# Hybrid decoder layer on one core: other waiting steps in the attention and ahead of the decay products, the keys' rate term on another engine, two small products in other banks

## The chip, the cores and the metric

The kernel runs on one core of a Trainium2 chip. The metric is the device time of one execution in microseconds (us); the time of a kernel is the median of its runs.

## The reference

A layer of width 2048 works on one sequence of 256 tokens in fp32. A first SwiGLU block of width 5632 is followed by a mixer, a cross attention into a memory of 256 tokens, a second SwiGLU block and a final norm. The mixer runs two token mixers beside each other, gates them and projects the sum:

```
h = rms_norm(x, norm_g)
p = h @ w_in
q, k, v, p_rwkv, gates = jnp.split(p, c, axis=-1)
y_attn = sliding_window_attention(q, k, v, sinks)
y_rwkv = rwkv7_time_mix(p_rwkv, mu, w0, w2, a0, a2, g2, k_k, k_a, r_k, ln_w, ln_b)
gate_attn, gate_rwkv = jnp.split(jax.nn.sigmoid(gates), 2, axis=-1)
merged = gate_attn * (y_attn @ w_proj_attn) + gate_rwkv * (y_rwkv @ w_proj_rwkv)
return x + merged @ w_out
```

The attention has 16 heads in four groups (`kv` 0 to 3), each group with one key and value head, a window of 128 tokens and a sink. In the RWKV-7 part the change touches the decay, the rate `a` and the keys:

```
w_log = -jax.nn.softplus(-(w0 + jnp.tanh(xw) @ w2)) - 0.5
a = jax.nn.sigmoid(a0 + xa @ a2)
g = jax.nn.sigmoid(xg) @ g2
kk = k * k_k
kk = kk / jnp.maximum(jnp.sqrt(jnp.sum(kk * kk, axis=-1, keepdims=True)), 1e-12)
k = k * (1.0 + (a - 1.0) * k_a)
```

The last line holds the keys' rate term, `1 + (a - 1) k_a`.

## The kernel before, in words

Every large product takes fp32 operands in two parts, hi and lo, and is done as three products of a faster form (lines L442 to L444 in `times`: hi·hi, lo·hi, hi·lo). Weights stream in through SyncE's queue (SP) as tiles `raw`; ScalarE (ACT) casts the hi part (L365) and VectorE (DVE) subtracts the lo part (L366), both in the order in which TensorE (PE) uses them. This stream is the backbone of the kernel.

All other work stands in generators. After each `multiply` (six of those products on one bank) the function `product` calls `bg.tick()`, and each waiting generator does its piece up to its next `yield`. Such a piece is a step; `idle(n)` lets n steps pass. Generators stand in groups with a limit: of the group "attn" two run at a time, of "ew" one. On top of this the build layer arranges the rows of each engine by its own estimates.

PSUM has three tags: `acc` (three banks, the stream's sums), `mm` (three) and `tr` (two, for transposes and small products). A row that writes a bank waits until ACT or DVE has emptied it.

The places of the change, in order of the program:
- `attend(kv)`, L938 to L1030, once for each head group: scores (L954, in `tr` and `mm`), bias and maximum on DVE (L962, L974), exponentials on ACT (L984), their normalising on DVE (L993), transposes on PE (L1003), copies of them on ACT (L1007, `pt`), the product with the values on PE (L1014), and its split into hi and lo (L1024 on ACT, L1025 on DVE). It idles at L945 before the scores and at L996 before the transposes.
- `decay_and_rate`, L1072 to L1130: when the attention has been issued, GpSimd (POOL) starts two DMAs for the weights `wa` (L1078, L1079); ACT does the tanh of `xwa` and the sigmoid of `xg` (L1081, L1082); PE then does two blocks of eight products per bank tag (L1091) and ACT their sigmoids (L1098).
- `gate_parts`, L1141: three copies of a part of `xg` by DMA, also issued by POOL (L1144).
- `removal_keys(h)`, L1163 to L1232, for two halves h: `kk` scaled on ACT (L1172), normalised on DVE (L1184, L1186), the products with decay and rate (L1190 to L1197), the keys' rate term (L1202), its use (L1206, L1207), products (L1216) and their masking (L1224).
- The gates: ACT's sigmoid (L1268), and DVE's product `ga` (L1271), which empties an `acc` bank of the stream.
- The RWKV pairs: masked scores (`mk`, L1348 on PE, L1356 on DVE); the bank taken at L1449 holds the products of L1459 to L1472. `finish` (L1486 to L1534) takes a bank for the product with the gate's weights, L1523.

Of the kernel before, what the change touches and what calls it, by code (L numbers as in the profile page):

```python
# [9 lines left out]
AF = mybir.ActivationFunctionType  # L10
ALU = mybir.AluOpType
# [125 lines left out]
def decoder_layer(ctx: ExitStack, tc: tile.TileContext, a: dict, out: bass.AP):  # L137
    nc = tc.nc
    act, dve, pool, pe = nc.scalar, nc.vector, nc.gpsimd, nc.tensor
# [17 lines left out]
    def f32(x):  # L157
        return x.bitcast(F32)
# [4 lines left out]
    def mm():  # L163
        return ps.tile([P, 512], F32, tag="mm", name="mm")

    def tr():
        return ps.tile([P, 512], F32, tag="tr", name="tr", bufs=2)
# [5 lines left out]
    def idle(n):  # L173
        for _ in range(n):
            yield
# [68 lines left out]
    w0, a0, k_k, k_a, r_k, ln_w, ln_b = (cols[:, 80 + i * 8 : 88 + i * 8] for i in range(7))  # L244
    mu = cols[:, 136:163]
    nk_k = cpool.tile([P, 8], F32, name="nk_k")
    ok_a = cpool.tile([P, 8], F32, name="ok_a")
# [22 lines left out]
    for entry in weight_plan(a):  # L270
# [10 lines left out]
        for k in range(k0, k0 + nk, 2 * KU):  # L281
            u = len(units)
            units += [(v, k + i, c, 512) for v, c in zip(w, c0) for i in (0, KU)]
            for i in range(2):
                q = (k - k0) // KU + i
# [587 lines left out]
    with tc.tile_pool(name="mx", bufs=1, reuse_waits="tile") as sp:  # L873
# [66 lines left out]
        def attend(kv):  # L940
            yield from wait_for("kv")
            if kv == 0:
                with tc.issue_after(at["features"].ins):
                    act.activation(junk_t[:, :1], ones[:, :1], AF.Exp)
            yield from idle(5 * (kv % 2))  # L945
            s, b = [], []
            for qb, bank in enumerate((tr, mm)):
                w, tq = P * (qb + 1), slice(qb * P, qb * P + P)
# [9 lines left out]
            for qb in range(2):  # L958
                w = P * (qb + 1)
                bias = abias[:, 1 - qb :, :].rearrange("p a b -> p (a b)")  # L960
# [30 lines left out]
            for qb in range(2):  # L991
                for i in range(4):
                    dve.tensor_scalar(  # L993
                        s3[qb][:, i], s3[qb][:, i], den[:, qb, i : i + 1], None, ALU.mult
                    )
            yield from idle(3)  # L996
            pt = []
            for qb in range(2):
                pt.append(t4("pt", (P, 2, 4, P)))
# [71 lines left out]
        cs, ee, e0, aa, at_, bt, dec = [], [], [], [], [], [], []  # L1071
        keep2 = keep[:].rearrange("p c t -> p (c t)")  # L1072

        def decay_and_rate():
            yield from wait_for("small")
            yield from wait_for("attn")
            wa = t4("wa", (P, RW))
            pool.dma_start(wa[0:64, :], W["rwkv_w2"])  # L1078
            pool.dma_start(wa[64:128, :], W["rwkv_a2"])  # L1079
            with tc.issue_after(at["exp"].ins):  # L1080
                act.activation(xwa[0:64, :], xwa[0:64, :], AF.Tanh)  # L1081
                act.activation(xg[:], xg[:], AF.Sigmoid)  # L1082
            yield
            for h in range(2):
                cs.append(t4("cs"))
                aa.append(t4("aa"))
                b = [[bank() for _ in range(2)] for bank in (mm, tr)]
                for i in range(4):
                    for e in range(2):
                        r, c = slice(64 * e, 64 * e + 64), (4 * h + i) * P  # L1090
                        pe.matmul(  # L1091
                            b[i // 2][e][:, i % 2 * T : (i % 2 + 1) * T], wa[r, c : c + P],
                            xwa[r, :], start=True, stop=True,
                        )
                for i in (2, 3, 0, 1):
                    for e, (dst, bias) in enumerate(((cs[h], w0), (aa[h], a0))):
                        c = 4 * h + i
                        sigmoid = act.activation(  # L1098
                            dst[:, i, :], b[i // 2][e][:, i % 2 * T : (i % 2 + 1) * T], AF.Sigmoid,
                            bias=bias[:, c : c + 1],  # L1100
                        )
                yield from idle(4)
            for h in range(2):
                for c in range(4):
                    dve.tensor_tensor_scan(
                        cs[h][:, c, :], keep2, cs[h][:, c, :], 0.0, ALU.mult, ALU.add
                    )
                    if c % 2:
                        yield
                c3 = halves(cs[h])  # L1110
                mid = stat.tile([P, 8], F32, tag="mid", name="mid")
                dve.tensor_copy(mid[:], c3[:, :, 63])
                dve.tensor_tensor(
                    c3, c3, mid[:].unsqueeze(2).to_broadcast([P, 8, P]), ALU.subtract
                )
                dec.append(stat.tile([P, 4], F32, tag="dec", name="dec"))
                dve.tensor_tensor(dec[h][:], cs[h][:, :, 127], mid[:, 1:8:2], ALU.add)
                yield
                with tc.issue_after(sigmoid.ins):
                    act.activation(dec[h][:], dec[h][:], AF.Exp, scale=-DECAY)  # L1120

                ee.append(t4("ee", (P, 8, P)))
                e0.append(stat.tile([P, 8], F32, tag="e0", name="e0"))
                with tc.issue_after(sigmoid.ins):
                    act.activation(e0[h][:], mid[:], AF.Exp, scale=DECAY)
                    act.activation(ee[h][:], c3, AF.Exp, scale=-DECAY)
                yield
                act.activation(cs[h][:], cs[h][:], AF.Exp, scale=DECAY)
                yield
            bg.seen.add("decay")  # L1130
# [34 lines left out]
        def removal_keys(h):  # L1165
            yield from wait_for(f"k{h}")
            yield from wait_for("decay")
            ei = cs[h]
            kk, sq = t4("kk"), t4("sq")
            for i in range(4):  # L1170
                c = 4 * h + i
                act.activation(kk[:, i, :], kt[h][:, i, :], AF.Copy, scale=nk_k[:, c : c + 1])  # L1172
            yield
            act.activation(sq[:], kk[:], AF.Square)
            yield
            for i in (0, 2):
                b = tr()
                sq2 = sq[:, i : i + 2, :].rearrange("p c t -> p (c t)")
                pe.matmul(b[:], bdones[:], sq2, start=True, stop=True)
                act.activation(sq2, b[:], AF.Sqrt)  # L1180
                yield
                dve.tensor_scalar(sq2, sq2, 1e-12, None, ALU.max)
                for k in range(2):
                    dve.reciprocal(sq[:, i + k, :], sq[:, i + k, :])  # L1184
                    yield from idle(2)
            dve.tensor_tensor(kk[:], kk[:], sq[:], ALU.mult)  # L1186
            yield
            at_.append(t4("at"))
            for later, before in ((slice(1, P), ee[h][:, :, : P - 1]), (0, e0[h][:])):
                dve.scalar_tensor_tensor(  # L1190
                    halves(at_[h])[:, :, later], halves(kk)[:, :, later], DOWN, before,
                    ALU.mult, ALU.mult,
                )
            yield
            dve.scalar_tensor_tensor(kk[:], kk[:], -1.0, aa[h][:], ALU.mult, ALU.mult)
            yield
            dve.tensor_tensor(kk[:], kk[:], ei[:], ALU.mult)  # L1197
            bt.append(kk)
            yield
            for i in range(4):  # L1200
                c = 4 * h + i
                dve.tensor_scalar(  # L1202
                    aa[h][:, i, :], aa[h][:, i, :], k_a[:, c : c + 1], ok_a[:, c : c + 1],
                    ALU.mult, ALU.add,
                )
            dve.tensor_tensor(kt[h][:], kt[h][:], aa[h][:], ALU.mult)  # L1206
            dve.tensor_tensor(aa[h][:], kt[h][:], ei[:], ALU.mult)  # L1207

            lt = t4("lt", (P, 8, P))
            b = [[bank() for _ in range(2)] for bank in (tr, mm)]  # L1210
            for c in range(2):
                cs_ = slice(c * P, (c + 1) * P)
                for j in range(4):
                    for e in range(2):
                        r = slice(64 * e, 64 * e + 64)
                        pe.matmul(  # L1216
                            b[c][e][:, j * P : (j + 1) * P], at_[h][r, j, cs_], bt[h][r, j, cs_],
                            start=True, stop=True,
                        )
            for c in range(2):  # L1220
                lt = lt if c == 0 else t4("lt", (P, 8, P))
                yield
                for e in range(2):
                    dve.tensor_tensor(  # L1224
                        lt[:, 4 * e : 4 * e + 4, :], b[c][e][:].rearrange("p (j s) -> p j s", j=4),
                        mask_l[:].unsqueeze(1).to_broadcast([P, 4, P]), ALU.mult,
                    )
                o = h * 16 + c * 8
                pool.dma_start(ld[:, o : o + 8, :], lt[:])
                yield  # L1230
            yield
# [131 lines left out]
        def pairs(h, q):  # L1363
# [11 lines left out]
            for c in range(2):  # L1375
# [9 lines left out]
                b = tr()  # L1385
# [13 lines left out]
                b = tr()  # L1399
# [29 lines left out]
                if c == 0:  # L1429
                    b = mm()  # L1430
# [15 lines left out]
                if c == 0:  # L1446
                    mk_next = masked(scores(h, js, ((0, 1), (1, 1)), tr), mask3[:, :2])
                    yield
                b = tr()  # L1449
                if c:  # L1450
                    for k, j in enumerate(js):
                        pe.matmul(
# [36 lines left out]
        def finish(h, i):  # L1489
# [16 lines left out]
            b = head_sums(bdmean, sp_)  # L1506
# [6 lines left out]
            gl = sp.tile([P, 2 * P], F32R, tag="gl", name="gl", bufs=1)  # L1513
            dve.tensor_tensor(gl[:], g2[:, 0, :], f32(gh[:, 0]), ALU.subtract)
            dve.tensor_tensor(gh[:64, 1], g2[:64, 1, :], f32(gh[:64, 1]), ALU.subtract)
            yield from idle(2)
            b = tr()
            for k in range(2):
                o, fk = b[:, k * T : (k + 1) * T], slice(k * P, (k + 1) * P)
                for m, (g_, x_) in enumerate((  # L1520
# [132 lines left out]
        for h in (0, 2):  # L1653
            b = tr()
# [129 lines left out]
```

## Time and profile before

| | us |
|---|---|
| median of 3 runs | 2225.18 (2224.05 to 2226.93) |
| profiled execution | 2226.33 |
| its span | 2224.6 |
| PE busy | 2206.0 |
| DVE busy | 1831.3 |
| ACT busy | 1244.2 |
| POOL busy | 107.2 |

The profile is of one execution, so numbers from it go with 2226.33; 1.73 us of that lie around the span. Busy time counts an engine as busy however slow its clock; PE's granted clock has a column of its own in the views of windows. A row of a timeline gives start, duration, engine, line, what is written and read, and in brackets the idle time ahead of it with what ended it.

### The profile page before, as it was taken

The numbers are of one execution on the slowest core, as the hardware profiler recorded it, in microseconds if no ns is written. First come the engines' busy times: TensorE is split into PE (matmuls) and PEld (weight loads), VectorE is DVE, ScalarE is ACT, GpSimd is POOL, SyncE is SP. The second block draws the span as 40 slices with busy tenths as digits, with TensorE's granted clock in tenths as the row PEclk, the third lists the DMA queues.
The fourth block names the chain that finished last, engine by engine and source line by source line (L and its number), as shares of the span: only waits on it lengthen the run. The fifth ranks groups of instructions, "written<-read, shape, count | busy, mean of one in ns | idle before, by whom it ended". The sixth has DMA issues, their size and how long they took to land.

```text
span 2224.6 us, 28133 instructions
## 1 busy us (share of the span) xinstructions
PE 2206.0 (99%) x10520; PEld 1819.2 (82%) x10520; DVE 1831.3 (82%) x2354; ACT 1244.2 (56%) x1611; POOL 107.2 (5%) x185
## 2 busy tenths in 40 slices
PE   9999999999999999999999999999999999999998
PEld 7888888888888877788888888888888888888886
DVE  7999988898989476978657666558999999999997
ACT  7555555555556467544544546556665565655654
POOL 0000000000000001000221030001000000000000
PEclk9999999999999999999999999999999999999999
DMA  8565555555556545676678678548565565656573
GB/s 304 194 209 198 194 203 199 201 191 202 203 192 202 175 126 149 191 235 209 205 236 293 203 265 281 186 157 288 206 234 189 197 247 204 208 208 218 199 242 137
DMA packets 231560, 466.02 MB, mean 209 GB/s; under 512 B 15520, under 2 KB 17920, under 8 KB 231424
## 3 DMA queue, kind: packets, MB, share of 16 engines
q1 hardware_dynamic: 222256, 438.08, 58.0%
q0 software_dynamic: 7648, 23.52, 3.5%
q10 hardware_dynamic: 1520, 2.63, 0.3%
q8 instruction: 82, 1.34, 0.2%
q14 instruction: 54, 0.44, 0.1%
HBM read 440.49 MB, written 23.59 MB: 209 GB/s over the span
## 4 chain that ended last, share of the span: by engine, by line
PE 94%; DVE 2%; DMA 1%; issue 1%; ACT 1%; SPq 0%; POOL 0%; POOLq 0%; DVEq 0%; ACTq 0%
PE acc L442 19%; PE acc L443 19%; PE acc L444 19%; PE mm L443 8%; PE mm L444 8%; PE mm L442 8%; PE tr L443 2%; PE tr L630 2%; PE tr L442 2%; PE tr L444 2%; PE mm L1418 1%; DVE lo L366 1%; DMA raw<-in_ffn_w_up_dram 0%; ACT hi L365 0%; DMA raw<-in_ffn_w_gate_dram 0%
## 5 line engine op out<-in xcount | busy, mean ns | idle before, releaser
L365 ACT CAST hi<-raw 128x1024 fp32r<-128x1024 f32 (+1 forms) x768 | 754.9, 993 | 698.3 <-PE acc L444 493.6
L366 DVE TENSOR_TENSOR lo<-raw,hi 128x1024 fp32r<-128x1024 f32 (+1 forms) x768 | 880.7, 1150 | 291.7 <-ACT hi L365 288.9
L442 PE MATMUL acc<-hi,xhi 128*128 128x512 f32 (+1 forms) x1134 | 448.1, 396 | 2.8 <-DVE ga L1271 1.3
L443 PE MATMUL acc<-lo,xhi 128*128 128x512 f32 (+1 forms) x1134 | 440.6, 389 | 0.8 <-DVE lo L366 0.8
L444 PE MATMUL acc<-hi,xlo 128*128 128x512 f32 (+1 forms) x1134 | 440.5, 389 | 0.0
L442 PEld LDWEIGHTS acc<-hi,xhi 128*128 128x128 f32 x1134 | 213.3, 188 | 49.2 <-issue 3.6
L443 PEld LDWEIGHTS acc<-lo,xhi 128*128 128x128 f32 x1134 | 213.6, 188 | 44.2 <-DVE lo L366 2.1
L444 PEld LDWEIGHTS acc<-hi,xlo 128*128 128x128 f32 x1134 | 213.2, 188 | 44.1 <-issue 0.8
L373 ACT CAST thi<-raw 128x1024 fp32r<-128x1024 f32 x192 | 200.2, 1051 | 67.5 <-DVE raw L396 44.1
L374 DVE TENSOR_TENSOR tlo<-raw,thi 128x1024 fp32r<-128x1024 f32 x192 | 232.5, 1219 | 0.9 <-ACT thi L373 0.3
L442 PE MATMUL mm<-hi,xhi 128*128 128x512 f32 x402 | 156.5, 389 | 0.0
L443 PE MATMUL mm<-lo,xhi 128*128 128x512 f32 x402 | 156.5, 389 | 0.0
L444 PE MATMUL mm<-hi,xlo 128*128 128x512 f32 x402 | 156.4, 389 | 0.0
L444 PE MATMUL acc<-hi,hlo 128*128 128x512 f32 x372 | 145.4, 391 | 0.0
L443 PE MATMUL acc<-lo,hhi 128*128 128x512 f32 x372 | 145.3, 391 | 0.0
L442 PE MATMUL acc<-hi,hhi 128*128 128x512 f32 x372 | 145.0, 390 | 0.0
L442 PEld LDWEIGHTS mm<-hi,xhi 128*128 128x128 f32 x402 | 75.5, 188 | 16.2 <-ACT hi L365 0.5
L443 PEld LDWEIGHTS mm<-lo,xhi 128*128 128x128 f32 x402 | 75.5, 188 | 15.8
L444 PEld LDWEIGHTS mm<-hi,xlo 128*128 128x128 f32 x402 | 75.5, 188 | 15.7
L442 PEld LDWEIGHTS acc<-hi,hhi 128*128 128x128 f32 x372 | 69.9, 188 | 14.3
L443 PEld LDWEIGHTS acc<-lo,hhi 128*128 128x128 f32 x372 | 69.8, 188 | 14.2
L444 PEld LDWEIGHTS acc<-hi,hlo 128*128 128x128 f32 x372 | 69.9, 188 | 14.1
(421 smaller groups left out, 3527.9 us busy)
## 6 DMA issues: line engine op xcount, KB each, us to landing
raw<-in_ffn_w_down_dram SPq DMA_DIRECT2D x88, 1024.0 KB, 5.2
raw<-in_ffn_w_gate_dram SPq DMA_DIRECT2D x84, 1024.0 KB, 5.0
raw<-in_ffn_w_up_dram SPq DMA_DIRECT2D x78, 1024.0 KB, 5.9
raw<-in_w_in_dram SPq DMA_DIRECT2D x136, 512.0 KB, 3.7
raw<-in_w_out_dram SPq DMA_DIRECT2D x32, 512.0 KB, 4.6
raw<-sums SPq DMA_DIRECT2D x20, 512.0 KB, 6.3
raw<-in_w_proj_attn_dram SPq DMA_DIRECT2D x16, 512.0 KB, 4.1
raw<-in_w_proj_rwkv_dram SPq DMA_DIRECT2D x16, 512.0 KB, 5.3
```

What stands on the lines that cost most here:

```text
L365: at["hi"] = act.copy(hi[:, s], raw[:, s])
L366: at["lo"] = dve.tensor_tensor(lo[:, s], raw[:, s], f32(hi[:, s]), ALU.subtract)
L373: act.copy(hi[:], v[:])
L374: dve.tensor_tensor(lo[:], v[:], f32(hi[:]), ALU.subtract)
L442: pe.matmul(o, xh, hi, start=first, stop=False, **how)
L443: pe.matmul(o, xh, lo, start=False, stop=False, **how)
L444: pe.matmul(o, xl, hi, start=False, stop=last, **how)
L630: pe.transpose(b[:, o : o + P], tok[:, t, col : col + P], ident[:])
L1418: pe.matmul(vb[to, (o + k) * P : (o + k + 1) * P][:, r], lhs(k, e), v[:, k, r], start=v is u and k + e == 0, stop=True, **ek,)
```

## The change

Five edits:
- The fourth head group (`kv` 3) no longer idles five steps before its scores; the second still does.
- The first head group idles five steps instead of three before its transposes.
- After the two DMAs for `wa`, five steps pass before the tanh, the sigmoid and the products.
- The keys' rate term is done by ACT (Identity with scale and bias), four operations per half, instead of by DVE.
- Two small products take an `mm` bank instead of `tr`: at L1449 for one pair, at L1517 for the first `finish`, which also idles one step instead of two.

```
-            yield from idle(5 * (kv % 2))
+            yield from idle(5 * (kv == 1))
...
-            yield from idle(3)
+            yield from idle(5 if kv == 0 else 3)
...
             pool.dma_start(wa[64:128, :], W["rwkv_a2"])
+            yield from idle(5)
             with tc.issue_after(at["exp"].ins):
...
-                dve.tensor_scalar(
-                    aa[h][:, i, :], aa[h][:, i, :], k_a[:, c : c + 1], ok_a[:, c : c + 1],
-                    ALU.mult, ALU.add,
+                act.activation(
+                    aa[h][:, i, :], aa[h][:, i, :], AF.Identity, scale=k_a[:, c : c + 1],
+                    bias=ok_a[:, c : c + 1],
                 )
...
-                b = tr()
+                b = mm() if h == q == 1 and c == 0 else tr()
...
-            yield from idle(2)
-            b = tr()
+            yield
+            b = mm() if h == i == 0 else tr()
```

One line is added, so the lines of the changed kernel from L1080 on stand one number higher.

How the rows move, first on POOL, around the requests for `wa`; a row is line, operation, what is written and read, and the shape:

```order
 L1040 MEMSET p 128x2 x2
-L1144 DMA xg<-xg 32x256 x2
+L1145 DMA xg<-xg 32x256
 L1078 DMA wa<-in_rwkv_w_dram 64x1024
 L1079 DMA wa<-in_rwkv_a_dram 64x1024
+L1145 DMA xg<-xg 32x256 x2
 L1047 TENSOR_TENSOR d<-p 128x512 x2
-L1144 DMA xg<-xg 32x256
 L1040 MEMSET p 128x2 x2
```

One copy of `xg` stands ahead of the requests instead of two, and the other two follow them.

Then ACT, from the third head group's exponentials to the sigmoid of `xg`. Before:

```order
L984 ACTIVATE s,den<-s,nm 128x128 x3
L984 ACTIVATE s,den<-s,nm 128x256 x4
L1024 CAST yahi<-tr 128x512
L365 CAST hi<-raw 128x1024 x2
...
L365 CAST hi<-raw 128x1024 x2
L981 ACTIVATE es<-es 128x8
L984 ACTIVATE s,den<-s,nm 128x128 x4
L984 ACTIVATE s,den<-s,nm 128x256 x4
L365 CAST hi<-raw 128x1024 x2
L1007 COPY pt<-tr 128x512
L1081 ACTIVATE xwa<-xwa 64x256
L1082 ACT_TABLE_LOAD
```

And now:

```order
L984 ACTIVATE s,den<-s,nm 128x256 x4
L365 CAST hi<-raw 128x1024 x2
L1007 COPY pt<-tr 128x512
L984 ACTIVATE s,den<-s,nm 128x128
L981 ACTIVATE es<-es 128x8
L984 ACTIVATE s,den<-s,nm 128x128 x3
L984 ACTIVATE s,den<-s,nm 128x256 x4
L1007 COPY pt<-tr 128x512 x2
L365 CAST hi<-raw 128x1024
L1082 ACTIVATE xwa<-xwa 64x256
L1024 CAST yahi<-tr 128x512
L1083 ACT_TABLE_LOAD
```

The fourth group's exponentials now stand between the first and the other two of the third group's copies of transposed weights.

Last, DVE in the first half of the removal keys, from the product with the decay to `ga`. Before:

```order
L1197 TENSOR_TENSOR kk<-kk,cs 128x1024
L1202 TENSOR_SCALAR aa<-aa,cols,ok_a 128x256 x4
L366 TENSOR_TENSOR lo<-raw,hi 128x1024
L1206 TENSOR_TENSOR kt<-kt,aa 128x1024
L1224 TENSOR_TENSOR lt<-tr,mask_l 128x512
L1207 TENSOR_TENSOR aa<-kt,cs 128x1024
L1224 TENSOR_TENSOR lt<-tr,mask_l 128x512
L1224 TENSOR_TENSOR lt<-mm,mask_l 128x512 x2
L1271 TENSOR_TENSOR ga<-acc,ga 128x512 x2
```

And now:

```order
L1198 TENSOR_TENSOR kk<-kk,cs 128x1024
L1207 TENSOR_TENSOR kt<-kt,aa 128x1024
L366 TENSOR_TENSOR lo<-raw,hi 128x1024
L1208 TENSOR_TENSOR aa<-kt,cs 128x1024
L1225 TENSOR_TENSOR lt<-tr,mask_l 128x512 x2
L1225 TENSOR_TENSOR lt<-mm,mask_l 128x512 x2
L1272 TENSOR_TENSOR ga<-acc,ga 128x512 x2
```

The four operations of the rate term are gone from DVE, and `ga` stands that much earlier. On PE the first product into the bank that the second `ga` empties stood behind 13 products of the next tile pair into the other bank, and stands behind 7 now. PE does the same 9989 operations; the eight decay products of the first block keep their place in its order.

## The prediction

> **What bounds the kernel now.** I read the page first, then the list of PE's waits, then windows around the longest of them.
>
> ```profile
> PE 2206.0 (99%) x10520; PEld 1819.2 (82%) x10520; DVE 1831.3 (82%) x2354; ACT 1244.2 (56%) x1611; POOL 107.2 (5%) x185
> ```
>
> PE is busy in 2206.0 of a span of 2224.6 us. A change that leaves the products alone can win only three things: PE's waits, a clock below full, and what an interruption of the matmul stream costs. The waits:
>
> ```profile
> engine line waited for: us in total, times, longest us
> PE mm L1091 <- DMA wa<-in_rwkv_w_dram: 2.0, 1, 2.0
> PE tr L1003 <- DVE s L993: 1.6, 1, 1.6
> PE acc L442 <- DVE ga L1271: 1.3, 2, 0.7
> ...
> PE tr L1523 <- DVE mk L1356: 0.7, 1, 0.7
> PE tr L1014 <- ACT pt L1007: 0.4, 1, 0.4
> PE tr L1459 <- DVE mk L1356: 0.3, 1, 0.3
> ```
>
> The rows shown add up to 6.3 us, all in the mixer; the longest is the decay products waiting for their weights. Windows show what follows that wait (columns: length, busy time of PE, PEld, DVE, ACT, POOL, granted clock, DMA share, GB/s).
>
> ```profile
> 844.42:846.94 2.52, 0.49 (x3) 0.19 (x2) 1.53 (x2) 1.53 (x2) 1.44 (x2) 1.00 0.99 204
> 847.95:854.80 6.85, 6.85 (x21) 5.09 (x21) 4.58 (x10) 3.24 (x8) 0.20 (x2) 0.50 0.29 88
> 854.80:858.40 3.60, 3.60 (x17) 2.97 (x16) 2.29 (x3) 1.05 (x1) 0.00 (x0) 1.00 0.02 5
> 791.00:797.00 6.00, 4.42 (x34) 4.00 (x32) 5.53 (x18) 3.62 (x11) 0.00 (x0) 1.00 0.51 153
> ```
>
> Right behind the 2.0-us wait the granted clock is 0.50 for 6.85 us, with PE "busy" all the while: a loss that no list of waits holds. At half speed 6.85 us hold 3.43 us of work, so 3.4 us are lost. The 1.6-us wait, inside the last window, is followed by no such drop: the point from which a wait costs the clock lies between 1.6 and 2.0 us here, or depends on where the wait falls.
>
> **The change part by part.** *The weights of decay and rate (the first three edits).* Two timelines, of PE and of POOL, and two pieces of the chain:
>
> ```profile
> 843.24 1.25 PE L1014 MATMUL tr<-pt,vt 128*64 128x256 f32 x10
> 844.42 0.49 PE L444 MATMUL acc<-hi,xlo 128*128 128x512 f32 x1
> 846.94 1.79 PE L1091 MATMUL mm<-xwa,wa 64*128 64x256 f32 x5 [2.03 <-DMA wa<-in_rwkv_w_dram]
> ```
>
> ```profile
> 839.47 1.06 POOL L1144 DMA_DIRECT2D xg<-xg  x2 [24.57 <-ACT xg L1082]
> 840.52 0.53 POOL L1078 DMA_DIRECT2D wa<-in_rwkv_w_dram  x1
> ```
>
> ```profile
> 838.54 0.64 ACT xg L1082
> ...
> 840.52 6.38 DMA wa<-in_rwkv_w_dram
> ```
>
> PE is ready at 844.91 (846.94 less 2.03). The weights are asked for at 840.52 and land 6.38 us later. POOL would have asked sooner, but two copies of xg stand ahead in its queue and they wait for ScalarE's sigmoid of 838.54. So the question is when that sigmoid runs after the change. On ScalarE it stands behind the exponentials of the last head group, which lose five idle steps; a step is six products of 512 columns, which start 0.23 us apart (6 × 0.2275 = 1.37 us):
>
> ```profile
> 914.58 0.39 PE L444 MATMUL acc<-hi,xlo 128*128 128x512 f32 x1
> 914.81 0.39 PE L442 MATMUL acc<-hi,xhi 128*128 128x512 f32 x1
> 915.85 0.50 PE L442 MATMUL acc<-hi,xhi 128*128 128x512 f32 x1 [0.65 <-DVE ga L1271]
> ```
>
> Four steps are 5.5 us; three, if ScalarE's denser queue eats one, 4.1. One copy of xg instead of two stands ahead, which is 0.5 of the 1.06 us. The request then leaves between 840.52 − 4.1 = 836.4 and 840.52 − 6.0 = 834.5, and lands between 840.9 and 842.8, or about 2 to 4 us before PE is ready. The attention itself delivers PE a little earlier (next paragraph), about 0.2 us net. So the wait goes whole: −2.0. With no gap there the clock stays up: −3.4. The second half of the weights, which PE waited for within the same block, comes with it:
>
> ```profile
> its engine sat idle before it (us, times) until:
>   DMA wa<-in_rwkv_w_dram: 4.4, 2
>   issue: 0.4, 1
>   DMA wa<-in_rwkv_a_dram: 0.3, 1
> ```
>
> That is the view of line L1091, matmuls and weight loads together; −0.3 from its last row. What hides the transfer is attention work on PE; if that cover is gone, each us of lateness is a us of wait. Next late behind it are the sigmoids on ScalarE, which PE doesn't wait for within the block.
>
> [...]
>
> *Denser attention.* By the two orders, PE goes from 23 to 17 interruptions of the fp32r stream by other products in this stretch. The price of one, from the spacing of starts:
>
> ```profile
> 798.21 0.29 PE L444 MATMUL acc<-hi,xlo 128*128 128x288 f32 x1
> 798.43 1.13 PE L954 MATMUL mm<-kd,qt 64*128 64x256 f32 x8
> 799.50 0.40 PE L442 MATMUL acc<-hi,xhi 128*128 128x288 f32 x1
> 799.74 0.29 PE L443 MATMUL acc<-lo,xhi 128*128 128x288 f32 x1
> 799.87 0.29 PE L444 MATMUL acc<-hi,xlo 128*128 128x288 f32 x1
> ```
>
> Products of 288 columns start 0.13 apart (799.74 to 799.87). Entering the excursion takes 0.22, leaving it 0.24: about 0.2 too much in all. Six fewer are −1.2; the bounds are 0.5, if only one side is saved, and 1.8, if the excursions at 512 columns cost half again as much.
>
> Against it stand new waits. The third and fourth head groups now run nearly together, and on ScalarE the fourth's exponentials stand between the third's first copy of transposed weights (L1007) and its other two. They last from 830.82 to 834.43 in the trace before:
>
> ```profile
> 830.82 0.39 ACT L984 ACTIVATE s<-s,nm 128x128 f32<-128x128 f32 x1
> ...
> 834.24 0.20 ACT L984 ACTIVATION_READ_ACCUMULATOR s<-s,nm 128x1 f32 x1
> ```
>
> So the third group's later copies can come up to 3.6 us late, and PE stands at L1014 for what the rows in between don't cover. Those are 17 products at 0.23, or 3.9 us, and eight transposes: more than the exponentials. The nearest row is the 0.4 us that L1014 waits for L1007 before. I take three small waits of 0.2 to 0.5, 1.0 in all; bounds 0 and 2.0. The first group's 1.6-us wait keeps its place: nothing ahead of it changes on PE, DVE or ScalarE up to there. Nothing is claimed for it.
>
> *The keys' rate term.*
>
> ```profile
> 908.02 1.38 DVE L1202 TENSOR_SCALAR aa<-aa,cols,ok_a 128x256 f32<-128x256 f32 x4
> ...
> 915.11 1.28 DVE L1271 TENSOR_TENSOR ga<-acc,ga 128x512 f32<-128x512 f32 x2
> ```
>
> ```profile
> 952.15 0.50 PE L442 MATMUL acc<-hi,xhi 128*128 128x512 f32 x1 [0.62 <-DVE ga L1271]
> ```
>
> ```profile
> 912.28 1.06 ACT L365 CAST hi<-raw 128x1024 fp32r<-128x1024 f32 x1 [3.88 <-DVE lt L1224]
> 913.25 1.70 ACT L1172 ACTIVATE kk<-kt,nk_k 128x256 f32<-128x256 f32 x4
> ```
>
> For each of the two halves DVE loses 1.3 us between the removed work and the product ga that frees PE's bank. ScalarE has room: its four operations, by its own scaling copies of the same shape 1.70 us, fall near a stretch of 3.88 us in which it sat idle. In the second half PE's order doesn't change: the 0.62 goes, −0.6 (bound 0, if a cast that now stands behind the new operations is late). In the first half PE's rows that need the bank moved six matmuls ahead, 1.37 us, as much as DVE gained. So its 0.65 stays: 0, bounds −0.65 and +0.3.
>
> *Two small products in other banks.*
>
> ```profile
> 1174.75 0.50 PE L1523 MATMUL tr<-xr,gh 128*128 128x256 f32 x2 [0.74 <-DVE mk L1356]
> 1225.45 0.44 PE L1459 MATMUL tr<-mk,vtok 128*64 128x128 f32 x4 [0.31 <-DVE mk L1356]
> ```
>
> Both waited for DVE to empty a transpose bank. In an mm bank both waits go, −0.74 and −0.31. But L1523 now comes a step earlier, which reorders DVE's finish work ahead of the pair's own copies; between nothing and 0.7 comes back there. I take −0.4 for the first (bounds −0.74 and +0.1) and −0.3 for the second.
>
> **The sum.** −2.0 − 3.4 − 0.3 − 1.2 + 1.0 − 0.6 − 0.4 − 0.3 = −7.2. The profiled execution took 2226.33 us, 1.73 of them around the span, and 2226.33 − 7.2 = **2219.1**; I say 2219.0. The median of the runs shown is 1.15 lower, perhaps because the clock drop isn't in each of them; from the median the sum would give 2218.0. At best (all lower bounds: −2.0 − 3.4 − 0.3 − 1.8 − 0.6 − 0.65 − 0.74 − 0.3, no new wait) it is 2216.5; with 2.0 of new waits and 0.5 for the interruptions 2220.8.
>
> **Rivals.**
> - [...] Chance 0.20.
> - *The change doesn't do what it says*: the request stays behind a copy of xg that waits for the sigmoid, ScalarE is held by the denser attention, and the weights land after PE's arrival again. For it: one copy still stands ahead. Against it: 2 to 4 us of slack. Decay wait and clock stay: −1.2 + 1.0 − 0.6 − 0.4 − 0.3 = −1.5, or 2224.8. Chance 0.13.
> - *Slower*: ScalarE's exponentials hold back the third group's copies by their whole 3.6 us, PE waits that long at L1014, the clock drops there as it did at L1091 (3.4), and since the sigmoid stands behind all this, the decay wait keeps its price too. That is +7.0 − 1.2 − 1.3 (the last three terms) = +4.5, or 2230.8. It decides when the uncovered wait passes 2.0 us and the request passes 844.7 − 6.4 = 838.3. For it: the copies really stand behind the exponentials. Against it: the 3.9 us of products in between. Chance 0.07.
>
> **How the numbers follow.** The forecast has the remaining 0.60. About 0.2% (4.45 us) is what a measurement of this kernel can tell from no change, so faster means below 2220.73 and slower above 2229.63. The forecast is nearly all below (0.57), the first rival rarely (0.03): faster 0.60. The rest of both and the second rival make same 0.33; slower 0.07. A range of 2216.5 to 2224.3 holds nearly all of forecast and first rival and a third of the second: 0.8.
>
> **What would show it.** Right: no row L1092 <- DMA wa among PE's waits; a granted clock of 1.00 through the stretch after the decay products; the first eight decay products in about 2 us; no wait behind ga in the second half; L1003's 1.6 still there, and the ga wait of the first half near 0.7. Wrong: a wait over 1.6 us at L1014 or L1003 of the third or fourth head group with half clock behind it; the request for wa issued after 838; or half clock at a place without a wait.

## The result and the profile after

The changed kernel takes 2217.84 us (median of 7 runs, 2217.41 to 2218.98), the kernel before 2226.51 beside it (7 runs, 2221.94 to 2228.11). The ratio is 0.9966, with a 95% interval of 0.9954 to 0.9977: faster by 0.34%. Forecast were 2219.0, and faster by over 0.2%. What also changed is the spread: 1.6 us after, 6.2 before.

The profiled execution after took 2218.01 us with a span of 2216.3. The page's busy line for the engines and the list of PE's waits:

```profile
PE 2201.2 (99%) x10520; PEld 1817.0 (82%) x10520; DVE 1826.4 (82%) x2346; ACT 1248.4 (56%) x1619; POOL 107.0 (5%) x185
```

```profile
engine line waited for: us in total, times, longest us
PE tr L1003 <- DVE s L993: 1.6, 1, 1.6
PE mm L187 <- POOL ones L183: 1.1, 1, 1.1
PE acc L442 <- ACT hi L365: 1.0, 1, 1.0
PE acc L443 <- DVE lo L366: 0.8, 2, 0.5
PE acc L442 <- DVE ga L1272: 0.7, 1, 0.7
PE acc L442 <- ACT hi L669: 0.6, 1, 0.6
PE tr L1014 <- ACT pt L1007: 0.3, 1, 0.3
```

The wait on `wa` is gone, one of the two on `ga`, and those at L1523 and L1459. The waits of the first head group (1.6 and 0.3) remain. No new one came: the rows of L187, L365, L366 and L669 stand in the first 25 us, ahead of the mixer, and were there before too, with 1.1, 0.3, 0.8 and 1.2. ScalarE's sigmoid, POOL's requests, PE's rows at the decay products and two windows behind them (length, busy PE, granted clock, DMA share, GB/s):

```profile
830.04 0.63 ACT L1083 ACTIVATE xg<-xg 128x512 f32<-128x512 f32 x1
```

```profile
830.96 0.56 POOL L1145 DMA_DIRECT2D xg<-xg  x1 [8.33 <-ACT xg L1083]
831.60 0.54 POOL L1078 DMA_DIRECT2D wa<-in_rwkv_w_dram  x1
```

```profile
842.94 0.39 PE L444 MATMUL acc<-hi,xlo 128*128 128x512 f32 x1
843.26 1.14 PE L1092 MATMUL mm<-xwa,wa 64*128 64x256 f32 x8
844.22 1.03 PE L1092 MATMUL tr<-xwa,wa 64*128 64x256 f32 x8
```

```profile
847.00:850.40 3.40, 3.40 (x17) 1.00 0.43 147
850.40:853.80 3.40, 3.40 (x23) 1.00 0.15 14
```

The sigmoid started 8.5 us earlier than before (830.04 for 838.54) and the request left 8.9 us earlier (831.60 for 840.52). The weights landed 3.6 us later, 8 us ahead of their products; these follow the stream without a gap, and the clock stays at 1.00.

Both programs have 10520 matmul records, so the same product, counted from the first, can be looked up in both traces. The table gives its start before, and after minus before:

```
start before    after - before   since the row above
  790.13            +0.05
  802.68            -0.17        -0.22  first two head groups
  844.42            -1.48        -1.31  rest of the attention
  847.26            -4.00        -2.52  the wait on wa
  858.77            -7.88        -3.88  behind it, to the second block of decay products
  948.20            -7.91        -0.03  keys, first half
  955.01            -8.48        -0.57  keys, second half
 1228.17            -8.85        -0.37  pairs and first finish
 1330.01            -9.01        -0.16
 2200.04            -8.26        +0.75  cross attention and second SwiGLU
```

### The profile page after: what moved, and what is told of

It reads as the page before. It is cut to its first block, busy times and chain, and to the rows that moved or that the text cites. A ratio compares the mean times of both kernels' runs of the same rounds, so it can differ in the third digit from the quotient of the medians.

```text
span 2216.3 us, 28136 instructions
## 1 busy us (share of the span) xinstructions
PE 2201.2 (99%) x10520; PEld 1817.0 (82%) x10520; DVE 1826.4 (82%) x2346; ACT 1248.4 (56%) x1619; POOL 107.0 (5%) x185
## 4 chain that ended last, share of the span: by engine, by line
PE 94%; DVE 3%; DMA 1%; ACT 1%; issue 1%; SPq 0%; POOLq 0%; POOL 0%; DVEq 0%; ACTq 0%
PE acc L442 19%; PE acc L443 19%; PE acc L444 19%; PE mm L444 8%; PE mm L443 8%; PE mm L442 8%; PE tr L630 2%; PE tr L443 2%; PE tr L442 2%; PE tr L444 2%; PE mm L1419 1%; DVE lo L366 1%; DMA raw<-in_ffn_w_up_dram 1%; PE tr L1349 0%; DMA raw<-in_ffn_w_gate_dram 0%
## 5 line engine op out<-in xcount | busy, mean ns | idle before, releaser
L365 ACT CAST hi<-raw 128x1024 fp32r<-128x1024 f32 (+1 forms) x768 | 755.0, 993 | 691.6 <-PE acc L444 491.1
L366 DVE TENSOR_TENSOR lo<-raw,hi 128x1024 fp32r<-128x1024 f32 (+1 forms) x768 | 879.4, 1148 | 293.4 <-ACT hi L365 291.0
```

What stands on the lines that cost most here:

```text
L365: at["hi"] = act.copy(hi[:, s], raw[:, s])
L366: at["lo"] = dve.tensor_tensor(lo[:, s], raw[:, s], f32(hi[:, s]), ALU.subtract)
```

## The experiments

Theory A: the time came from the decay products' wait, the half clock behind it, and fewer interruptions in the attention. Rivals: the last two edits carry half of it (B); half clock has another cause than the gap (C); the length of the gap decides, not its place on the grid of 3.413 us on which the clock changes in these traces (D).

**First three edits alone** (e1), **last two alone** (e2).

```
e1, before with
+ idle(5 * (kv == 1)) ... idle(5 if kv == 0 else 3) ... idle(5) after the DMAs of wa
e2, before with
+ act.activation(aa[h][:, i, :], ..., AF.Identity, scale=..., bias=...) ... mm() at L1449 and L1517, one idle step there
```

> The kernel before with the first three edits alone (the idle steps of the attention and of the decay generator). Theory A (the time came from the decay products' wait, the half clock behind it and the denser attention): all but about 1 us of the change's 8.7, so about 2218.8 us, no wait on the weights wa and a granted clock of 1.00 behind the decay products; the ga waits of 0.65 and 0.62 and the waits at L1523 and L1459 are still there. Rival B (the rate term on ScalarE and the banks bring half of it): about 2222.

> The kernel before with the last two edits alone (rate term on ScalarE, two products in mm banks). Theory A: 0.5 to 1.0 us below before, about 2225.7, with the 2.0-us wait on wa and half clock behind it as before; the wait of the second ga is gone, that of the first stays near 0.7. Rival B: about 2222, and then the waits removed are worth more than their length.

e1 took 2219.25 us (2218.56 to 2219.74), ratio to before 0.9973 (0.9962 to 0.9983): 1.4 us above the changed kernel, where theory A had 1.0. No wait on `wa` is left, and those on `ga` (0.65 and 0.66), at the first `finish` (0.73) and at the pair (0.31) are still there. e2 took 2222.89 in the median, but from 2221.36 to 2227.17, ratio 0.9992 (0.9983 to 1.0001). The median alone would speak for B. The mean granted clock of each run separates them: seven runs at 0.999 have a median of 2221.7, three at 0.998 of 2225.5, one at 0.997 took 2227.17. So e2's median is that of runs without the clock's drop. At the same clock, 0.999, fifteen runs of before beside it have a median of 2223.8, so e2 is 2.1 lower: more than A's 1.0, and less than the half of the change, 4.3, that B asks for. By its trace the keys bring 0.6 and the banks 0.5; what the other 1.0 is stays open. Its profile was one with a drop, and an instructive one, by PE's row and two windows:

```profile
847.33 0.72 PE L1091 MATMUL mm<-xwa,wa 64*128 64x256 f32 x1 [1.82 <-DMA wa<-in_rwkv_w_dram]
```

```profile
847.70:851.10 3.40, 3.40 (x14) 0.54 0.70 196
851.10:854.50 3.40, 3.40 (x16) 1.00 0.00 1
```

Here half clock lasts one stretch of 3.4 us, where the profile of before had two. The runs of the kernel before fall into such groups as well. Its 64 different times beside e1 to e12 are, by their mean clock: 34 at 0.999 (median 2223.5), 12 at 0.998 (2225.9), 18 at 0.997 (2227.0). No profile with a mean of 0.999 has half clock in the mixer; e2's, at 0.998, has one stretch, and those of before at 0.997 have two. The mean is rounded, so the middle group may be mixed. In about half of the runs of before nothing was lost to the clock.

**Only the request moved** (e4). The rows of PE, ScalarE and VectorE stand as before.

```
+            wa = t4("wa", (P, RW)); pool.dma_start(...) x2
             yield from wait_for("attn")
-            wa = t4("wa", (P, RW)); pool.dma_start(...) x2
```

> The kernel before with one thing moved: the two DMAs for wa are written ahead of the wait for the attention. The rows of PE, ScalarE and VectorE stand in the same order as before; on POOL the requests stand ahead of the copies of xg. Theory A (the gap causes the half clock): no wait on wa, granted clock 1.00 throughout the mixer, 2.0 + 3.7 = 5.7 us less, about 2220.8, and runs that lie closer together. Rival C (half clock has another cause in this stretch, such as the transposes and small products of the attention): only the wait goes, about 2224.5, and half clock of some 6.8 us is still there.

2220.97 us (2220.37 to 2222.24), ratio 0.9981 (0.9972 to 0.999); all eleven runs at a mean clock of 0.999. The windows at the decay products:

```profile
843.00:847.00 4.00, 4.00 (x31) 1.00 0.55 163
847.00:850.40 3.40, 3.40 (x18) 1.00 0.42 110
```

With the attention's order untouched and the gap gone the half clock is gone too: C falls. Against the profile of before the same product starts 2.40 earlier right behind the wait and 3.74 more at the second block, and nothing else moves until 1330. Between e4 and e1 lies the denser attention: from 790 to the last product ahead of the decay products 1.5 us by the same products, and 1.7 in the medians.

**The request made late again in the new order** (e5): fills of `wa` ahead of its DMAs.

```
             wa = t4("wa", (P, RW))
+            for _ in range(12): pool.memset(wa[:], 0.0)
```

> The changed kernel with twelve fills of the tile wa by POOL ahead of its requests (0.97 us each by the fills of the same shape at L1242), so that the weights land late again in the new order; the decay products stand a few products later on PE. Theory A: a wait of 1 to 4 us at the decay products; if it is over 2, granted clock of 0.50 for 3.4 or 6.8 us behind it and a time of 2217.8 + wait + 1.7 to 3.7, some 2221 to 2225. Rival C: the clock stays at 1.00 and the time is 2217.8 + wait alone, 2219 to 2222.

2226.49 us (2226.01 to 2227.92), 8.65 above the changed kernel; ratio to before 1.0005 (0.9996 to 1.0014). Not one of its ten runs has a clock of 0.999.

```profile
851.02 0.45 PE L1094 MATMUL mm<-xwa,wa 64*128 64x256 f32 x1 [2.96 <-DMA wa<-in_rwkv_w_dram]
```

```profile
852.50:859.40 6.90, 6.90 (x26) 0.52 0.02 4
```

One late transfer gives back the whole change. The time lies above both expectations. From the same product in the profile of the changed kernel, 7.5 us are lost between 842 and 855 and 0.6 behind 1260. Of the 7.5, 2.96 are the wait and 6.90 us at 0.52 another 3.3; the remaining 1.2 lie around the decay products, which stand later in this order and in other company. That last part wasn't tested. Theory A's price of the clock holds (3.3 for its 1.7 to 3.7), and C is out for this order too.

**Three more profiles of the kernel before** (e6, e7, e12; no edit).

> The kernel before, unchanged, profiled once more. Theory A with the grid: the gap at the decay products is again about 2.0 us; what half clock follows depends on where the gap falls in windows of 3.41 us, so this look shows no half clock (span about 2221), one window of it (about 2223) or two (2224.6), and the length of the gap doesn't differ between them. Rival D (the gap itself differs between executions, by the time that the DMA takes): where there is no half clock the gap is well under 1.8 us.

> The same as the look before it, a second time: theory A and rival D as there. The two looks together should show at least one other length of half clock than 6.8 us if the spread of this kernel's runs (2221.8 to 2228.0) comes from it.

> The kernel before once more. Theory D: half clock if the gap at the decay products is 1.8 us or more, none if it is below 1.58. Rival A: the two don't go together.

2226.46, 2223.87 and 2227.13 us. e7's profile has no half clock, and its gap is shorter:

```profile
846.50 0.48 PE L1091 MATMUL mm<-xwa,wa 64*128 64x256 f32 x1 [1.37 <-DMA wa<-in_rwkv_w_dram]
```

```profile
844.00:847.00 3.00, 1.63 (x11) 1.00 0.95 248
847.00:850.40 3.40, 3.40 (x20) 1.00 0.57 157
```

And e12, the shortest gap with half clock behind it:

```profile
846.82 0.48 PE L1091 MATMUL mm<-xwa,wa 64*128 64x256 f32 x1 [1.62 <-DMA wa<-in_rwkv_w_dram]
```

```profile
847.00:850.40 3.40, 3.40 (x14) 0.59 0.68 182
850.40:853.80 3.40, 3.40 (x9) 0.50 0.08 31
```

e6's gap was 1.81, with half clock. So theory A's clause that the gap doesn't differ between executions fell: the four profiles of this kernel have gaps of 2.03, 1.81, 1.62 and 1.37, which follow the time from the request (840.52, 840.45, 840.79, 840.74) to the products: 6.4, 6.2, 6.0 and 5.8. That is what D says of the gaps, with a single profile (e7) on the side without half clock. e12 lies in the stretch between 1.58 and 1.8 that D had left open.

**Gaps of other lengths in the old order** (e10, e11).

```
             wa = t4("wa", (P, RW))
+            pool.memset(wa[:], 0.0)                        # e10 once; e11 twice, and
+            pool.memset(wa[:, :128], 0.0)                  # e11 this
```

> The kernel before with one fill of wa by POOL (0.97 us) ahead of its requests, and all three copies of xg ahead of them (0.5 more); PE has twelve products of the stream more ahead of the decay products (2.7 us). Theory D (the length of the gap decides the half clock, from a point between 1.58 and 1.81 us): a gap of 2.0 + 1.5 - 2.7 = 0.8 us, at most 1.2, no half clock, and every run at the clock of the undisturbed ones (0.999), about 2222.5. Rival A (the place in the windows of 3.41 us decides): some runs at 0.997 or 0.998 still.

> The same with two whole fills and one of an eighth: 1.1 us more, a gap of about 1.9 us, between 1.3 and 2.2 as the transfer takes 5.7 to 6.4. Theory D: half clock in the profile exactly if its gap is over 1.6 to 1.8; the runs fall in two or three groups as those of the kernel before do, by their mean clock. Rival A: a gap over 1.8 without half clock, or one below 1.58 with it.

e10: 2222.44 us (2221.28 to 2223.44), all ten runs at 0.999, as D has it. Its gap was 0.40, half of what was expected:

```profile
846.26 0.45 PE L1093 MATMUL mm<-xwa,wa 64*128 64x256 f32 x1 [0.40 <-DMA wa<-in_rwkv_w_dram]
```

e11: 2229.11 us (2227.64 to 2229.9), its ten runs at 0.996 and 0.997, so not in the groups of the kernel before. Its gap was 3.03, not 1.9: the request left 1.5 us after e10's (843.61 for 842.14), not 1.1, and from there to the products it took 6.3 us, e10's 4.1.

```profile
849.93 0.45 PE L1094 MATMUL mm<-xwa,wa 64*128 64x256 f32 x1 [3.03 <-DMA wa<-in_rwkv_w_dram]
```

In the profiles, gaps of 0.40 and 1.37 dropped no clock and gaps of 1.62 to 3.03 did. Of the other runs only the mean clock is known: all ten of e10 are at 0.999, and all twenty of e5 and e11 at 0.998 or below. So the length counts. The place counts too, which D denied, and the traces show how. In all fourteen profiles every change of the clock lies a whole number of 3.413 us behind the first one (by the clock records of the trace before 843.09, 849.92 and 2215.25 us, or 247, 249 and 649 times 3.413; of the one after 2205.01 us, or 646 times). Windows of e11's profile on this grid, first at the decay products, then at L1003 (length, busy PE, granted clock, DMA share, GB/s):

```profile
844.95:848.36 3.41, 1.94 (x9) 1.00 0.97 251
848.37:851.78 3.41, 1.85 (x12) 1.00 0.72 198
851.78:855.19 3.41, 3.41 (x11) 0.50 0.00 0
```

```profile
793.75:797.17 3.42, 1.84 (x14) 1.00 0.22 36
797.17:800.58 3.41, 3.41 (x27) 1.00 0.79 244
```

The gap of 3.03 falls into two windows. Behind the first, with 1.47 us of it, the clock stays at 1.00; behind the second, with 1.56, it drops to 0.50. e5's gap of 2.96 is cut the same way, into 1.38 and 1.59, and its clock is 1.00 up to 852.5 and 0.52 in the 6.90 us behind. The gaps of before, e2, e6, e7 and e12 lie whole in one window each. So at the decay products the half clock goes with PE's idle time within one window of 3.41 us: with 1.47 or less it never came, with 1.56 or more it came in all six profiles.

The wait at L1003 fits only to within 0.03 us: in ten profiles its 1.58 lies whole in one window, as in the last two rows, and no drop follows. Whether that is the accuracy of the trace, in which the ends of matmuls are modelled, or PE's other work in the window counts as well, is open; so is why e2 lost one stretch and the others two. An estimate from these figures takes 1.57 us as the point. At a random place on the grid a gap of 2.03 us would be cut into two harmless parts in (2 × 1.57 − 2.03) / 3.41 = 0.33 of the executions, one of 1.62 in 0.45 and one of 3.03 in 0.03. So the runs of before without half clock can come from the place as well as from shorter gaps; no run separates the two.

**The largest wait left** (e8, e9).

```
-            yield from idle(5 if kv == 0 else 3)
+            yield from idle(6 if kv == 0 else 3)      # e9: 8
```

> The changed kernel with six idle steps instead of five ahead of the first head group's transposes. On PE the first transposes then stand four products of 288 columns later (4 x 0.13 = 0.5 us), so the largest wait left, 1.6 us at L1003, should shrink to about 1.1 and the time fall by 0.5, to 2217.3. Rival: the copies behind it come later, and L1014 waits for what L1003 no longer does: 2217.8.

> The changed kernel with eight idle steps there. The first transposes stand 16 products later (2.1 us), so the 1.6-us wait at L1003 goes whole, but the values' products of the first two groups stand together and behind more copies. Theory: a new wait of up to 0.6 at L1014 and 2216.8. Rival: ScalarE's copies and exponentials are late for the twelve products, PE waits 1.6 us or more there, and the time is 2217.8 to 2218.5; over 1.7 us half clock would follow as well, 2220 or more.

Both expectations missed, and so did the rivals' explanations: 2219.5 and 2220.41 us, 1.7 and 2.6 above the changed kernel, though the wait shrank: to 1.0 in e8, as meant, and to 0.6 in e9, where new ones of 0.6 and 0.4 came later in the attention. The first rows of the waits, e8:

```profile
PE mm L187 <- POOL ones L183: 1.1, 1, 1.1
PE tr L1003 <- DVE s L993: 1.0, 1, 1.0
```

PE idles less than in the changed kernel (5.4 for 6.6 us, all gaps over the span) and the kernel is slower. Most of the loss is inside PE's busy time: where the scores stand. From the first score of a block to the next other product, two scores of 256 columns alone take 0.63 us, as this row pair of the profile before shows, four of 128 columns 0.64, and eight of 256 take 1.06 (798.43 to 799.50, shown in the prediction):

```profile
809.99 0.70 PE L954 MATMUL mm<-kd,qt 64*128 64x256 f32 x2
810.62 0.88 PE L630 MATMUL tr<-ident,tok 128*128 128x128 f32 x6
```

The 48 scores from 788 us on stand in 8 blocks before (6.8 us in all), in 4 after (5.6), in 6 in e8 (7.1, with a 0.34-us wait in it), in 8 in e9 (7.6).

**Scores split on purpose** (e13).

```
             for qb, bank in enumerate((tr, mm)):
+                if qb and kv > 1:
+                    yield
```

> The changed kernel with one more step between the two halves of the scores of the third and fourth head groups. On PE the scores of these groups then stand in five blocks instead of three. Theory E (a block of scores between products of the stream costs about 0.5 us however few products it holds, read from the starts in three traces): the scores alone take 2 x 0.5 = 1.0 us more from start to next start, the attention's end comes later by about that and the time is 2218.8. Rival: a block costs 0.2 us, as the prediction had it: 0.4 more, and 2218.2; what else moves in the attention's order adds to either.

2220.96 us (2219.57 to 2222.87). The 48 scores stand in 6 blocks and take 6.4 us, 0.8 more than in the changed kernel's 4: nearer to theory E's 1.0 than to 0.4. A block of two again takes 0.63:

```profile
803.77 0.70 PE L956 MATMUL mm<-kd,qt 64*128 64x256 f32 x2
804.40 0.50 PE L442 MATMUL acc<-hi,xhi 128*128 128x512 f32 x1
```

The attention's end comes only 0.5 us later, by the products at 858: the 0.34-us wait of the changed kernel at L1014 is gone in this order, and 0.84 less 0.34 is 0.50. The time missed both, since 2.0 us more came between 1100 and 1170, in the pairs, which no edit touched. As a measure of a block e13 holds, as a measure of the kernel's time it doesn't. No version tried beats the changed kernel.

## Why the prediction was right, step by step

- **Wait on the weights, −2.0.** Right: −2.2 from the last product ahead of it to the first decay product, −2.5 to the second. The mechanism held (the sigmoid earlier, one copy ahead), with more room than worked out: the request left at 831.60, not at 834.5 to 836.4, because the fourth group's exponentials start 8.8 us earlier (822.04 for 830.82) and the sigmoid comes right behind the third group's products.
- **Half clock and second half of the weights, −3.4 − 0.3.** Right for the profiled execution: −3.9 by the table, −3.74 in e4. With the term above that is −6.4, forecast −5.7. The prediction left open whether the length of a wait or its place decides; both do, through the idle time within one window (behind 1.47 us the clock stayed at 1.00, behind 1.56 it dropped to 0.50). And the rival with the chance of 0.20, in which the drop isn't won because most runs of before never had it (about 2222.4), was half right: it was missing in about half. The median of before moves from set to set, from 2224.1 to 2226.5. Against runs of before at 0.999 the change is worth 2223.5 − 2217.84 = 5.7 us, against those at 0.997 9.2; which of the two a measurement shows is the luck of its runs.
- **Denser attention, −1.2 + 1.0.** The mis-sized term: −1.5 instead of −0.2. The new waits came out at zero, since the 3.9 us of products covered the copies behind the exponentials. The 0.2 per interruption is only part of the price: a block of scores holds PE for 0.6 us even when it is two products, and four blocks fewer are 1.2 of the 1.5.
- **Keys.** Right: 0 in the first half, where the wait is 0.71 behind the moved rows, and −0.57 in the second, forecast −0.6; e2, with the last two edits alone, has −0.60 there.
- **Banks, −0.4 − 0.3.** The waits of 0.74 and 0.31 went, but only 0.37 stayed by 1228, 0.5 by 1330. The last 96 of the products of L1348 take 8.32 us, from start to next start; before they took 8.23 with the wait of 0.74 in it, or 7.49 without. So 0.8 is given back by a reordering that no list of waits shows. The last two edits alone do this: e2 has the same 8.32, and has gained 0.33 by 1228 and 0.49 by 1330.
- **The remainder**: +0.75 behind 1330, in two places (near 1345 and 2085) where two or three matmuls start 0.1 us late; e4 shows shifts there against before as well, without any edit nearby.

The sum was −7.2 and the two profiled executions differ by 8.3. Up to 1330 it was 9.0; the 0.75 lost behind that, which nothing in the prediction foresaw, brought the measured time nearer to the forecast. That part of the nearness is luck.

## What to carry to other kernels

A wait of PE is to be priced together with the granted clock behind it: here 1.6 to 2.0 us of waiting for a 256-KB transfer brought up to 3.4 us of lost clock with it, in about half of the runs, and spread them over 6 us. A request that stands in a queue behind something that waits for another engine is late by that engine's order: before, POOL stood idle for 24.57 us until ScalarE's sigmoid let the copies of xg go, and the request behind them left at 840.52. Moved in front of them (e4) it left at 815.85, and the wait and the lost clock went at once. And a smaller sum of waits is no gain by itself (in e8 PE idled 5.4 for 6.6 us, and the kernel took 1.7 us longer): look also at how often the order breaks the stream.

## What the runs showed of the hardware

- In the traces the clock changed only on a grid of 3.413 us. At the decay products half clock (0.50) came in the six profiles in which PE had been idle for 1.56 us or more within one such window (1.56, 1.59, 1.62, 1.81, 1.82, 2.03), not at 1.47 or less, nor behind the 1.58 at L1003, and lasted 3.4 us (e2) or 6.8. The gaps of 3.03 (e11) and 2.96 (e5), which a window's edge cut in two, counted by their parts: no drop behind 1.47 and 1.38, one behind 1.56 and 1.59.
- The same 256-KB transfer took 3.6 us from request to landing while the DMA engines were 0.84 busy in the changed kernel, and 6.4 at 1.01 in the one before; four executions of the kernel before differed by 0.7 us in it (5.7 to 6.4).
- The time of a block of scores (64 rows deep) between products of the stream hardly depends on its length at first: two of 256 columns 0.63, four of 128 columns 0.64, eight of 256 1.06.
